# Lag rows of an S5 mixer fetched from on-chip copies in channel-first order, and the transforms of the last two units placed ahead of the late part

## Chip, core and metric

One NeuronCore of a Trainium2 chip runs the kernel; nothing is shared with another core. The metric is the device time of one execution in microseconds (us), the median over several runs. Engines: TensorE (PE; PEld is its weight load), VectorE (DVE), ScalarE (ACT), GpSimd (POOL), and SyncE (SP), which here only issues DMAs. ScalarE and GpSimd have DMA queues of their own.

## The reference, cut to what matters

One layer over 1024 latent tokens of width 1024 and 256 context tokens: a bidirectional S5 mixer with GELU and GLU, then a SwiGLU feed-forward net (FFN). Both have RMSNorm ahead and adaLN (shift, scale, gate, each a product of SiLU(c) with `ada_w`). The mixer has 64 groups of 16 channels, each with 64 complex states in each direction:

```python
def s5_direction(u_ctx, u_lat, lam_re, lam_im, log_step, b_re, b_im, c_re, c_im):
    lam_bar = jnp.exp(lam * jnp.exp(log_step)[:, None])
    b_bar = ((lam_bar - 1.0) / lam)[..., None] * lax.complex(b_re, b_im)
    c_mat = lax.complex(c_re, c_im)
    def run(u, h0):
        bu = jnp.einsum('lgh,gnh->lgn', u, b_bar)
        bu = bu.at[0].add(lam_bar * h0)
        _, h = lax.associative_scan(_linear_combine, (broadcast lam_bar, bu), axis=0)
        return jnp.einsum('lgn,ghn->lgh', h, c_mat).real, h[-1]
    y_c, h_c = run(u_ctx, 0)
    y_l, _ = run(u_lat, h_c)
    return y_c, y_l
# mixer: y = forward + backward + d_skip*h;  g = gelu(y);  g * sigmoid(g @ w_glu + b_glu)
# FFN:   (silu(h @ w1) * (h @ w3)) @ w2;     then the final RMSNorm
```

## The kernel before, in words

**Chunks of eight.** The sequence is cut into 128 chunks of T = 8 tokens. Within a chunk the output is a product of the chunk's inputs with a Toeplitz matrix of *lag kernels* (15 lags, -7 to 7, of 16 x 16 for each group); across chunks a recurrence runs over 128 chunk states. A chunk's input to one group is 8 x 16 = 128 numbers, and these stand on the 128 partitions: position s in the chunk times channel h, in the order s*16 + h. The 64 groups make eight *units* of eight groups, and two units a *quarter* q.

**Stages.** Up to about 123 us a preamble makes powers of lambda, the input matrices (`BL1`, `BL2`, made out of `LB` by `bl_make` and turned by `bl_tr`), the modulated input `U` and each chunk's contribution to the state. Then `scan` is the recurrence: VectorE steps from chunk to chunk, six operations a step, until 221 us. Beside it the other engines work through `PROG1`, a list written out by hand; from 222 us on all engines work through `PROG2`, then the GLU and the FFN. The order of the instructions on each engine is the order of the lists: an operation that waits holds up what stands behind it on its engine.

**Names in the lists** (the number is a unit 0-7, for T half a unit 0-15, for K half a quarter, for C a quarter and a part; `run` takes a list apart):
- `A`: products of adaLN with `ada_w`, whose tiles SP loads (L523). `M`, `m`: rows and columns made of them.
- `C`: readout factors of a quarter and direction on GpSimd (`cl_ops`): three products, L77, with two adds. `HOWS` says for each add how it is made: `P` on TensorE by two products with the identity and a copy (L693, L694), `Y` by an accumulating DMA issued on GpSimd (L696), `E` on GpSimd (L77). `q`, `G`, `L` prepare C; `q2` holds `pw_sums(1)` too.
- `K`: the lag kernels of half a quarter on TensorE (`k_mats`: L842, L846, L850), copied from PSUM to SBUF by ScalarE (L854) and from there written to the DRAM tensor `kd` (L855, 120 KB in 128 rows); `O` zeroes a PSUM tile first (L804).
- `T`: `toeplitz`, the fetch of the lag rows of four groups, half a unit, from `kd` to a tile of `KQ` (L863 on SP, 256 KB, 512 rows of 512 bytes). `KQ` has four tiles: a unit takes two of them, and the unit after the next takes the same two.
- `F`: GpSimd fills the odd chunk states of a quarter that the recurrence steps over.
- `R`, `Z`, `z`: copies of states in turned order for the backward direction (L955 on ScalarE, L957 on VectorE), of the first half of the chunks, the second half, and all.
- `P`: first half of a unit: `states_mm` (L975) for chunks that have both directions early, and `x_mm` (L999), the product of `U` with the lag rows, for all chunks; `Y`: its copy from PSUM (L1057, ScalarE). `N`: the second half's `states_mm`; `D`: its add on VectorE. Units 0 to 5 are done so.
- `Q`: units 6 and 7 instead have x_mm and `states_all` (L988), all chunks at once, in the late part, with no `D`.
- `H`: gelu on ScalarE (L1066, or L1069 in two halves straight from PSUM for 6 and 7); `I`, `J`: transposes for the GLU (L1123) with their copies (L1125) and low parts; `g`: the GLU's products (L1163); `w`, `l`, `W`, `V`: loads of `w_glu` (SP) and casts of it; `x`: gates.

All DMAs of SP's and ScalarE's queues share eight semaphores in turn, in the order of the program: each waits for the landing of the one eight before it. GpSimd's have eight of their own.

## Time and profile before

| what | us |
|---|---|
| runs, median (lowest to highest) | 1009.99 (1006.97 to 1013.54) |
| the profiled execution | 1006.91 |
| its span | 1005.1 |
| TensorE busy | 952.8 |
| GpSimd busy | 748.7 |
| end of the recurrence on VectorE | 221.1 |
| N0 to the first product of the GLU | 222.8 to 251.9 |

The span is what the profiler saw from the first to the last instruction; the execution's own time is 1.8 us longer, the median of the runs 3.1 us longer than that execution. A row of a grouped answer reads: line, engine, operation, out<-in by the program's names, shapes, count | busy us, mean ns of one | idle time of that engine just ahead of them and what ended it. A row of the timeline reads: start, duration, engine, line, operation, count, and in brackets the idle time ahead of it. A matmul in fp32 is recorded as two records. A row of a table of stretches gives, for each engine, busy us and records, then the granted TensorE clock (1.00 is full), the DMA engines' mean busy share, and GB/s.

### The profile page before, as it was taken

The numbers are of one execution on the slowest core, as the hardware profiler recorded it, in microseconds if no ns is written. First come the engines' busy times: TensorE is split into PE (matmuls) and PEld (weight loads), VectorE is DVE, ScalarE is ACT, GpSimd is POOL, SyncE is SP. The second block draws the span as 40 slices with busy tenths as digits, with TensorE's granted clock in tenths as the row PEclk, the third lists the DMA queues.
The fourth block names the chain that finished last, engine by engine and source line by source line (L and its number), as shares of the span: only waits on it lengthen the run. The fifth ranks groups of instructions, "written<-read, shape, count | busy, mean of one in ns | idle before, by whom it ended". The sixth has DMA issues, their size and how long they took to land. (4 is left out here: it accounts for less than half of the span.)

```text
span 1005.1 us, 17726 instructions
## 1 busy us (share of the span) xinstructions
PE 952.8 (95%) x6604; PEld 751.5 (75%) x6604; DVE 774.3 (77%) x1630; ACT 427.7 (43%) x808; POOL 748.7 (74%) x595
## 2 busy tenths in 40 slices
...
GB/s 335 285 133 108 287 316 273 125 85 171 210 64 22 1 105 84 11 43 42 74 53 74 42 79 34 47 61 45 74 42 84 43 64 32 61 55 53 74 22 167
DMA packets 49118, 99.95 MB, mean 99 GB/s; under 512 B 4348, under 2 KB 18940, under 8 KB 47752
## 3 DMA queue, kind: packets, MB, share of 16 engines
...
## 5 line engine op out<-in xcount | busy, mean ns | idle before, releaser
L77 POOL TENSOR_TENSOR c<-rxc,c 128x512 fp32r<-128x512 f32 x127 | 166.0, 1320 | 52.3 <-ACT c L1305 51.5
L1364 PE MATMUL ut<-ra,c 128*128 128x512 f32 x400 | 155.7, 389 | 1.2 <-DVE ra L77 1.2
L1363 PE MATMUL ut<-ra,c 128*128 128x512 f32 x400 | 155.7, 389 | 0.2 <-ACT ra L1305 0.2
L1365 PE MATMUL ut<-ra,c 128*128 128x512 f32 x400 | 155.6, 389 | 0.0
L1305 ACT CAST c<-rxc 128x512 fp32r<-128x512 f32 x128 | 79.0, 622 | 147.6 <-PE xt L1658 53.0
L1658 PE MATMUL xt<-c,c 128*128 128x512 f32 x540 | 129.7, 389 | 0.0
L77 DVE TENSOR_TENSOR ru<-ru,xt 128x1024 f32<-128x1024 f32 x90 | 107.9, 1216 | 13.4 <-PE xt L1658 9.4
L1658 PEld LDWEIGHTS xt<-c,c 128*128 128x128 f32 x540 | 101.4, 188 | 21.0
L77 DVE TENSOR_TENSOR ru<-ut,ru 128x512 f32<-128x512 f32 x98 | 67.2, 686 | 44.1 <-PE ut L1365 38.6
L1364 PEld LDWEIGHTS ut<-ra,c 128*128 128x128 f32 x400 | 75.1, 188 | 17.1 <-POOL rxc L77 1.5
L1363 PEld LDWEIGHTS ut<-ra,c 128*128 128x128 f32 x400 | 75.1, 188 | 16.1 <-ACT ra L1305 0.6
L1365 PEld LDWEIGHTS ut<-ra,c 128*128 128x128 f32 x400 | 75.1, 188 | 15.6
L77 POOL TENSOR_TENSOR c<-ru,c 128x512 fp32r<-128x512 f32 (+1 forms) x39 | 58.8, 1507 | 10.1 <-ACT c L1305 5.7
L77 POOL TENSOR_TENSOR rxc<-rxc 128x512 f32<-128x512 f32 (+1 forms) x44 | 63.8, 1450 | 2.2 <-ACT rxc L671 0.6
L77 POOL TENSOR_TENSOR c<-rw,c 128x512 fp32r<-128x512 f32 (+1 forms) x28 | 37.4, 1337 | 37.5 <-ACT c L1305 37.5
L1363 PE MATMUL ut<-c,c 128*128 128x512 f32 x160 | 62.3, 390 | 0.8 <-DVE rxa L77 0.8
L1364 PE MATMUL ut<-c,c 128*128 128x512 f32 x160 | 62.3, 389 | 0.0
L1365 PE MATMUL ut<-c,c 128*128 128x512 f32 x160 | 62.2, 389 | 0.0
L1658 PE MATMUL ut<-c,c 128*128 128x512 f32 x216 | 51.9, 389 | 0.0
L77 DVE TENSOR_TENSOR ru<-ru,ut 128x512 f32<-128x512 f32 x76 | 47.3, 680 | 0.7 <-ACT ru L1712 0.5
L1658 PEld LDWEIGHTS ut<-c,c 128*128 128x128 f32 x216 | 40.5, 188 | 8.4
L587 PE MATMUL pv<-ru,c 128*64 128x160 f32 x512 | 41.4, 312 | 5.2 <-ACT c L450 2.0
...
## 6 DMA issues: line engine op xcount, KB each, us to landing
c<-in_ada_w SPq DMA_DIRECT2D x46, 256.0 KB, 5.9
rxc<-in_w SPq DMA_DIRECT2D x38, 256.0 KB, 2.9
rxc<-in_w SPq DMA_DIRECT2D x19, 512.0 KB
c<-c POOLq DMA_DIRECT2D x11, 512.0 KB, 5.7
ru<-in_w SPq DMA_DIRECT2D x11, 512.0 KB
rw<-in_w SPq DMA_DIRECT2D x11, 512.0 KB, 3.6
ra<-in_ada_w SPq DMA_DIRECT2D x10, 512.0 KB, 10.8
ra<-in_ada_w SPq DMA_DIRECT2D x18, 256.0 KB, 8.8
```

The costliest lines, as they stand in the source:

```text
L77: eng.tensor_tensor(out=o, in0=x, in1=y, op=op)
L587: PE.matmul(pv[64 * (i % 2):64 * (i % 2) + 64, ri, c0:c0 + 160], w[:, i, 64 * ri:64 * ri + 64], U[:, 8 * b + 4 * j + i], start=True, stop= ...
L1305: S.copy(o[0], x)
L1363: PE.matmul(pu, wh, bh, start=start, stop=False)
L1364: PE.matmul(pu, wh, bl, start=False, stop=False)
L1365: PE.matmul(pu, wl, bh, start=False, stop=stop)
L1658: PE.matmul(pd, w[:, cs_], b, start=j in (1, 2, 4) and n == 0, stop=n == 2, skip_group_check=j not in (1, 2, 4))
```

## The change

1. **Channel-first order.** The 128 rows of a chunk's input stand as h*8 + s. The host arrays `xT`, `ctxT`, `blk` and `sel` are laid out so, `LB`, `BL1`, `BL2` have their last two dimensions exchanged, and the copies and transposes that read them take other strides. Counts and sizes of the instructions stay.
2. **Lag rows from SBUF.** The sixteen writes to `kd` are gone. `k_mats` copies the two halves' lag kernels into two SBUF tiles `KX`, and `toeplitz(u, hq, eng)` fetches from these: two DMAs a call, each for one group, 64 KB in 128 rows of 512 bytes; in channel-first order the destination's partitions follow from 16 source partitions and 8 lags. That makes 64 DMAs in place of 16 fetches and 16 writes. `T` and `t` (groups of the quarter's first and second K) issue on SP, `e0` to `e3` and `f0` to `f3` on ScalarE, right behind K0 and K1. Tiles of `KQ` are taken as before, so T12, T13, t12, t13 (unit 6) wait until P4 has read unit 4's, and T14, T15, t14, t15 (unit 7) until P5 has read unit 5's.
3. **Adds of the readout.** `HOWS` has two `E` in the third quarter and the `P` in the fourth replaced by `Y`. Signs are moved so that no `Y` add needs a sign after it. `pw_sums(1)` has two operations on GpSimd and one on ScalarE instead of four on GpSimd, as an entry of its own (`n1`) ahead of F10. C22 stands ahead of C21.
4. **Units 6 and 7.** `Q6`, `Q7` and the whole-length copies `z6`, `z7` go. `X6`, `X7` (their x_mm), the first halves `R6 S6 Y12 Y13`, `R7 S7 Y14 Y15` stand at the end of `PROG1`; `Z6 N6 D6`, `Z7 N7 D7` in `PROG2` make the second halves as for the other units, and one gelu of 128 x 1024 each replaces two.

The diff's core:

```diff
-HOWS = "YPYP EPEP YEYE YPYE"
+HOWS = "YPYP EPEP YYYY YYYE"
-PROG1 = ("A22 ... A34 K0 O1 A38 A42 C10 C11 K1 O2 L2 A46 A50 C12 C13 A54 K2 O3 A58 T0 T1 T2 T3 F10 F11 G2 R0 K3 L3 R1 P0 Y0 Y1 A64 M0 P1 T4 T5 R2 Y2 Y3 G3 q2 C20 T6 T7 C21 P2 R3 Y4 Y5 C22 M1 P3 Y6 Y7 C23 q3 C30 K4 K5 R4 T8 T9 T10 T11 C31 C32 C33 F30 F31 P4 R5 Y8 Y9 K6 P5 Y10 Y11 K7 T12 T13 T14 T15 w0 l1 M2 m0 w1")
+PROG1 = ("A22 ... A34 K0 e0 e1 e2 e3 O1 A38 A42 C10 C11 K1 O2 L2 f0 f1 f2 f3 A46 A50 C12 C13 n1 A54 K2 O3 A58 F10 F11 G2 R0 K3 L3 R1 P0 Y0 Y1 T4 T5 t4 t5 A64 M0 P1 R2 Y2 Y3 T6 T7 t6 t7 G3 q2 C20 C22 C21 P2 R3 Y4 Y5 M1 P3 Y6 Y7 C23 q3 C30 K4 T8 T9 T10 T11 K5 t8 t9 t10 t11 R4 C31 C32 C33 F30 F31 P4 R5 Y8 Y9 K6 T12 T13 K7 t12 t13 P5 Y10 Y11 T14 T15 t14 t15 w0 X6 X7 l1 M2 m0 w1 R6 S6 Y12 Y13 R7 S7 Y14 Y15")
-PROG2 = ("Z0 N0 Z1 Z2 D0 Z3 N1 D1 Z4 H0 H1 N2 D2 H2 N3 Z5 D3 H3 N4 D4 z6 z7 I0 J0 I1 J1 H4 N5 D5 I2 J2 H5 I3 J3 W0 W1 W2 W3 x0 x1 x2 x3 Q6 H6 I4 J4 Q7 I5 J5 V1 b0 w20 w21 l1 H7 g03 g13 ...")
+PROG2 = ("Z0 N0 Z1 Z2 D0 Z3 N1 D1 Z4 H0 H1 N2 D2 Z5 H2 N3 D3 Z6 H3 N4 Z7 D4 H4 I0 J0 N5 D5 I1 J1 H5 W0 W1 N6 D6 I2 J2 H6 I3 J3 W2 W3 x0 x1 x2 x3 N7 D7 I4 J4 H7 V1 b0 w20 w21 l1 I5 J5 g03 g13 ...")
...
-        LB = view(RC[2], 8, [2, T, P])
+        LB = view(RC[2], 8, [2, P, T])
...
-                    PE.transpose(pt[:, j, P * i:P * i + P], t1[:, 4 * j + i].rearrange("p s h -> p (s h)"), ident)
+                    PE.transpose(pt[:, j, P * i:P * i + P], t1[:, 4 * j + i].rearrange("p h s -> p (h s)"), ident)
...
-            tt(PS[i], PWF[:, :, 0, :, gs], PWF[:, :, 1, :, gs], ADD, E)
-            if i == 0:
-                tt(PWF[:, :, 1, :, gs], PWF[:, :, 1, :, gs], PWF[:, :, 0, :, gs], SUB, E)
-            else:
-                for d, gs, neg in ((slice(0, 2), slice(16, 24), True), (slice(0, 1), slice(24, 32), False), (slice(1, 2), slice(24, 32), True)):
-                    re, im = PWF[:, :, 0, d, gs], PWF[:, :, 1, d, gs]
-                    tt(im, re if neg else im, im if neg else re, SUB, E)
+            re, im = PWF[:, :, 0, :, gs], PWF[:, :, 1, :, gs]
+            tt(PS[i], im, re, SUB if i else ADD, E)
+            tt(im, im, re, ADD if i else SUB, E)
+            if i:
+                S.activation(im, im, AF.Copy, scale=-1.0)
...
-            tt(c2, c0, c1, SUB, E)
+            tt(c2, c0, c1, ADD if q > 1 else SUB, E)
...
-        KX = [cpk[:, HC + P:HC + P + 15 * HC], cols.rearrange("p a b g -> p (a b g)")[:, 0:15 * HC]]
-        KX += [view(RW, 4 + i, [15 * HC]) for i in range(2)]
+        KX = [R0[:, 32 + P:32 + P + 30 * HC], view(RW, 4, [30 * HC])]
+        KX = [t.rearrange("p (g x) -> p g x", g=2) for t in KX]
-        KD_ = [dr.tile([P, 4, 15 * HC], F32, tag=f"kd{q}", name=f"kd{q}") for q in range(4)]
...
-                gq, kx = 2 * hq + g_, KX[2 * hq + g_]
-                S.copy(kx, kts[g_])
-                S.dma_start(KD_[q][:, gq], kx)
-        def toeplitz(u):
-            q, gi = divmod(u, 4)
-            rows = KD_[q][32 * gi:32 * gi + HC]
-            n = 15 * HC
-            src = bass.AP(rows.tensor, rows.offset, [[HC, T], [n, 4 * HC], [1, P]])
-            SY.dma_start(KQ[u % 4], src)
+                S.copy(KX[hq][:, g_], kts[g_])
+        def toeplitz(u, hq, eng=SY):
+            for g_ in range(2):
+                rows = KX[hq][32 * (u % 4):32 * (u % 4) + HC, g_]
+                src = bass.AP(rows.tensor, rows.offset, [list(rows.ap[0]), [HC, T], [1, P]])
+                eng.dma_start(KQ[u % 4][:, 2 * hq + g_], src)
...
-        def states_all(k, pts, hs):
...
-        HSq = {6: view(RA, 0, [P, 2, 4]), 7: view(RA, STB, [P, 2, 4])}
...
-                    toeplitz(i)
+                elif op in "Ttef":
+                    toeplitz(i, int(op in "tf"), S if op in "ef" else SY)
...
-                    inner[i] = x_mm(i, pe8)
-                    states_all(i, inner[i], HSq[i])
+                elif op == "X":
+                    inner[i] = [pw([4, T, HC]), pw([4, T, HC]) if i == 6 else pm.rearrange("p (a t h) -> p a t h", a=4, t=T)]
+                    x_mm(i, inner[i], True)
+                elif op == "S":
+                    states_mm(i, inner[i], 0, HSe[i], False)
...
-                    if i in late:
-                        S.activation(Y[:, i], Y[:, i], AF.Gelu_apprx_tanh)
-                    else:
-                        for gp in range(2):
-                            S.activation(yview(i, gp), inner[i][gp], AF.Gelu_apprx_tanh)
+                    S.activation(Y[:, i], Y[:, i], AF.Gelu_apprx_tanh)
```

What this moves, at three places. In the changed kernel the same operations have other line numbers: L966 is the old L975 (states_mm), L975 the old L999 (x_mm), L1093 the old L1123 (transposes), L1133 the old L1163 (GLU), L850 the old L854, L1031 the old L1057, L946 the old L955, L857 the fetch.

First, TensorE from N0 to the GLU's first product. Before (a row of 64 L975 is two units):

```order
L975 MATMUL pe<-c_63,ra 64x128 x64
L975 MATMUL pe<-c_64,ra 64x128 x64
L975 MATMUL pe<-c_65,ra 64x128 x32
L1123 MATMUL pe<-r_60,ru 128x128 x8
L975 MATMUL pe<-c_65,ra 64x128 x32
L1123 MATMUL pe<-r_60,ru 128x128 x8
L999 MATMUL pe<-ra,ru 128x128 x8
L988 MATMUL pe<-c_66,ra 64x128 x64
L1123 MATMUL pe<-r_60,ru 128x128 x4
L999 MATMUL pe<-ra,ru 128x128 x8
L988 MATMUL pe<-c_66,ra 64x128 x64
L1123 MATMUL pe<-r_60,ru 128x128 x4
```

and in the changed kernel:

```order
L966 MATMUL pe<-c_63,ra 64x128 x64
L966 MATMUL pe<-c_64,ra 64x128 x64
L966 MATMUL pe<-c_65,ra 64x128 x32
L1093 MATMUL pe<-r_60,ru 128x128 x4
L966 MATMUL pe<-c_65,ra 64x128 x32
L1093 MATMUL pe<-r_60,ru 128x128 x4
L966 MATMUL pe<-c_66,ra 64x128 x32
L1093 MATMUL pe<-r_60,ru 128x128 x8
L966 MATMUL pe<-c_66,ra 64x128 x32
L1093 MATMUL pe<-r_60,ru 128x128 x8
L1133 MATMUL pe<-c_3321,c_3268 128x512
```

The two x_mm and the two whole state products are gone; two halves (c_66) stand in their place among the transposes.

Second, ScalarE behind K0 and K1. Before:

```order
L854 COPY r_60<-kt 128x240
L855 DMA kd_1250<-r_60 128x240
L854 COPY r_60<-pw 128x240
L855 DMA kd_1250<-r_60 128x240
L804 COPY pw<-r_60 128x240
L694 ACTIVATE c_64<-pw 128x512 x2
L854 COPY rw<-kt 128x240
```

and in the changed kernel:

```order
L850 COPY r_60<-kt 128x240
L850 COPY r_60<-pw 128x240
L857 DMA ra<-r_60 128x1x128 x8
L802 COPY pw<-r_60 128x240
L692 ACTIVATE c_64<-pw 128x512 x2
L850 COPY rw<-kt 128x240
L850 COPY rw<-pw 128x240
L802 COPY pw<-r_60 128x240
L665 DMA rxc<-in_cxy 128x512
L857 DMA ra<-rw 128x1x128 x8
L692 ACTIVATE c_64<-pw 128x512 x2
```

Eight issues of fetches stand ahead of the zeroing for K1 (L802), and eight more ahead of the second pair of copies of C's adds (L692).

Third, ScalarE at the end of `PROG1`, from K7's copies on, in the changed kernel:

```order
L850 COPY rw<-kt 128x240
L850 COPY rw<-pm 128x240
L1031 COPY ru<-pw 128x4x8x16 x2
L946 COPY ra<-ra 128x512
L1031 COPY ru<-pw 128x4x8x16 x2
L946 COPY ra<-ra 128x512
L1031 COPY ru<-pw 128x4x8x16
L1031 COPY ru<-pm 128x4x8x16
L946 COPY ra<-ra 128x512 x2
```

The copies of P5's result, R6, the copies of S6's result (Y12, Y13), R7, those of S7's (Y14, Y15), then the first copies of the late part on ScalarE (Z2, Z4). Before, K7's copies stood behind those of P5, and Z2 and Z4 right behind them.

70 lines of the change are left out of this document (26 added, 44 removed).

## The prediction

> **What bounds the kernel now.** I read the page first, then the table of stretches, then the stretch that the change shortens, group by group.
>
> ```profile
> span 1005.1 us, 17726 instructions
> PE 952.8 (95%) x6604; PEld 751.5 (75%) x6604; DVE 774.3 (77%) x1630; ACT 427.7 (43%) x808; POOL 748.7 (74%) x595
> ```
>
> 95% is an average over two regimes, which the stretches separate (each engine's busy us, then granted clock, DMA share, GB/s):
>
> ```profile
> 150.00:175.00 25.00, 21.97 (x563) 13.49 (x563) 25.00 (x144) 7.02 (x17) 22.12 (x26) 0.86 0.87 276
> 250.00:275.00 25.00, 25.00 (x166) 20.89 (x160) 11.70 (x12) 10.71 (x16) 19.21 (x10) 1.00 0.56 196
> ...
> 500.00:700.00 200.00, 200.00 (x884) 165.62 (x883) 141.71 (x169) 76.22 (x132) 156.47 (x118) 1.00 0.17 55
> ```
>
> Up to about 222 us VectorE is the bound: the recurrence, step after step, 25.00 busy of 25. From there on TensorE is: 200.00 of 200. The border is in the timeline of VectorE, followed there by the first copies of the late part (Z0, Z1):
>
> ```profile
> 220.82 0.29 DVE L77 TENSOR_TENSOR ra<-ltc,ra 128x128 f32<-128x128 f32 x1
> 221.25 0.76 DVE L957 COPY ra<-ra 128x512 f32<-128x512 f32 x2
> ```
>
> The late part begins with N0 (L975) and ends with the GLU's first product (L1163); by the answer on L975's line and by the timeline of TensorE:
>
> ```profile
> L975 PE MATMUL pe<-c,ra x384: 266/282/391, 222.8 to 237.2; 64*64 64x128 f32 x192
> ```
> ```profile
> 251.90 0.47 PE L1163 MATMUL pe<-c,c 128*128 128x512 f32 x1
> ```
>
> So a TensorE record taken out of 222.8–251.9 is worth its full time; one put in ahead of 222 costs nothing as long as TensorE is still through when the recurrence is. What that stretch holds, grouped by line (busy us, mean ns, idle before):
>
> ```profile
> L975 PE MATMUL pe<-c,ra 64*64 64x128 f32 x384 | 12.9, 285 | 1.3 <-issue 0.9 <-ACT rw L854 0.5
> L988 PE MATMUL pe<-c,ra 64*64 64x128 f32 x256 | 8.6, 288 | 0.4 <-issue 0.4
> L999 PE MATMUL pe<-ra,ru 128*128 128x128 f32 x32 | 3.9, 275 | 0.0
> L1123 PE MATMUL pe<-r,ru 128*128 128x128 f32 x24 | 3.5, 282 | 0.0
> ...
> ```
>
> 12.9 are N0 to N5, 8.6 and 3.9 are Q6 and Q7 whole, 3.5 the transposes; 29.1 us in all.
>
> **What the late part loses.** Q6 and Q7 go (8.6 + 3.9 = 12.5). N6 and N7 come: 128 records of the L975 kind, 12.9 × 128 / 384 = 4.3. Net **−8.2**, if TensorE stays fed: VectorE has two more pairs of adds (D6, D7; 4 × 0.69 = 2.8 us, against 6.6 of idle that it has before its adds), ScalarE one whole gelu (1.06) for each pair of half ones. From the same grouping:
>
> ```profile
> L77 DVE TENSOR_TENSOR ru<-pe,ru 128x512 f32<-128x512 f32 x12 | 7.7, 686 | 6.6 <-PE pe L975 6.5
> L1066 ACT ACTIVATE ru<-ru 128x1024 f32<-128x1024 f32 x6 | 6.4, 1061 | 4.1 <-DVE ru L77 3.9
> ```
>
> The turned copies of units 6 and 7 halve. I let the 1.7 us of idle stand. After 251.9 nothing is changed, and everything there waits for TensorE, so the end moves with the first GLU product. The w_glu loads are queued on SP behind the last lag fetch; SP is through with those fetches at 230 now (202.24 + 27.73 in its row below) and should be at 218 then, so they come earlier, too.
>
> **What the stretch ahead of it gains and loses.** X6, X7 and S6, S7 must now be done before N0. Their price: 3.9 (the L999 row) and 4.5 (128 records, first row below). What they replace and what room there is, TensorE in 190–222.8 by groups:
>
> ```profile
> L999 PE MATMUL pw<-ra,ru 128*128 128x128 f32 x45 | 7.8, 336 | 4.2 <-DMA ra<-kd 4.2
> L975 PE MATMUL pw<-c,ra 64*64 64x128 f32 x128 | 4.5, 287 | 0.0
> L693 PE MATMUL pw<-c,r 128*128 128x512 f32 x4 | 3.6, 1003 | 0.6 <-POOL c L77 0.6
> L693 PE MATMUL pw<-ra,r 128*128 128x512 f32 x4 | 2.9, 827 | 0.0
> ```
>
> The adds of the last readout product by TensorE (L693) go: about 6.0. That is 8.4 − 6.0 = 2.4 more work. The idle of that stretch is 6.7 (32.8 less 12.91, 6.84 and 6.33):
>
> ```profile
> 190.00:205.00 15.00, 12.91 (x353) 8.54 (x355) 15.00 (x86) 4.83 (x10) 14.25 (x10) 0.77 0.42 94
> 205.00:216.00 11.00, 6.84 (x147) 6.09 (x142) 10.79 (x59) 1.08 (x2) 10.77 (x14) 0.69 0.50 114
> 216.00:222.80 6.80, 6.33 (x287) 5.95 (x278) 5.85 (x30) 2.15 (x5) 3.12 (x7) 1.00 0.14 41
> ```
>
> So there is room, if the waits go. Why they are there: a lag kernel is written to DRAM, and the fetch of its rows waits for the landing.
>
> ```profile
> SPq L863 <- DMA kd<-r: 29.0, 2, 17.3
> L855 ACTq DMA_DIRECT2D kd<-r x8: 326/330/1498, 146.2 to 217.8; - x8
> DMA to landing us min/median/max: 2.7/3.3/5.0
> 202.24 27.73 SPq L863 DMA_DIRECT2D ra<-kd  x8
> PE pw L999 <- DMA ra<-kd: 4.2, 2, 3.6
> ```
>
> (SP's waits; the two kinds of kd; SP's timeline, eight fetches of 256 KB; TensorE's waits in 190–222.8.) The fetches for P4 and P5 go out from 202.24 on, and TensorE waits 3.6 for them at the longest. Now the fetch reads SBUF directly: no write, no landing in between. A new copy is 64 KB in 128 packets; nothing here has that form. Nearest is the write of 120 KB, also 128 packets: 0.33 us of issue and 2.7 to 5.0 to landing. I take 0.4 and 3; the lower bound is 2.7, the upper the old fetch. The rate while the last four of those run, in slices of 0.3 us from 225 on, is about 150 GB/s, 262 KB in 1.7 us, one after another:
>
> ```profile
> GB/s 6 27 0 0 0 55 17 9 0 137 174 174 176 140 132 119 147 114 193 137 116 150 126 164 164 225 176 241 251 207 224 203 215 241 253 239 246 205 423 410
> ```
>
> Step by step with these: the readout products on GpSimd come earlier. The third quarter loses two adds and gains two accumulating DMAs, the last one an add for a DMA:
>
> ```profile
> 175.54 2.02 POOL L77 TENSOR_TENSOR c<-rxc,rxa 128x1024 f32<-128x1024 f32 x1 [2.10 <-PE pm L534]
> 177.64 2.37 POOL L77 TENSOR_TENSOR c<-c,c 128x1024 f32<-128x1024 f32 x1
> ...
> 194.75 0.88 POOL L696 DMA_DIRECT2D c<-ra  x1 [0.30 <-POOL c L77]
> 204.94 2.35 POOL L77 TENSOR_TENSOR c<-c,rw 128x1024 f32<-128x1024 f32 x1
> ```
>
> Two adds of 2.37 less two issues of 0.88 + 0.30: 2.4 saved; one more DMA costs 1.2; and the 2.10 us of waiting ahead of 175.54 mostly go, since C22 is put ahead of C21. GpSimd ends the last product about 204 where it ended at 207.3. K4 stays near 191 and K5 near 195, since the landing of the last accumulation takes the place of the add:
>
> ```profile
> c<-c POOLq DMA_DIRECT2D x11, 512.0 KB, 5.7
> ```
>
> The fetches for P4 land about 201, eight us earlier. P4 and P5 are 2.2 of states and 2.0 of L999 each at full clock, a lag kernel about 2 (K7's copy starts at 222.39, P5's before it at 220.54; rows below). K6 needs the last accumulation, issued about 199.5, at 205 to 206. So P4 ends at 205 to 207, K6 at 207 to 208, K7 at 209 to 210.5, P5 at 213.5 to 215. **The last eight copies** (T14, T15, t14, t15) overwrite rows that P5 reads, so they go out only then: eight issues of 0.4 and 3 to landing, 219 to 221 for X7's end (X6 fits in between). S6: 2.2 (half of the 4.5). Then a wait that the order makes: R7, the turned copy that S7 reads, stands on ScalarE behind Y12 and Y13, and those wait for S6. From the timeline of ScalarE:
>
> ```profile
> 204.22 0.61 ACT L955 COPY ra<-ra 128x512 f32<-128x512 f32 x1
> ...
> 220.54 1.08 ACT L1057 COPY ru<-pw 128x512 f32<-128x512 f32 x2 [2.76 <-PE pw L999]
> 222.39 0.36 ACT L854 COPY rw<-kt 128x240 f32<-128x240 f32 x1 [0.78 <-PE pm L850]
> ```
>
> 1.08 + 0.61 and the signals: 1.9. S7: 2.2. So N0 starts at 220 + 2.2 + 1.9 + 2.2 = **226.3**, not 222.8: **+3.5**. Ends of it: 222.8 (recurrence and Z0 still last; a lower one isn't possible), and 238 if the copies cost what the old fetch did (the rival below).
>
> **The early copies** (e0–e3, f0–f3) are sixteen issues on ScalarE among the ada_w loads, where DMA share is 0.87. Each DMA waits for the one eight before it in program order, on whichever queue, and a load of 256 KB there takes 4.9 to land:
>
> ```profile
> c<-in_ada_w SPq DMA_DIRECT2D x13, 256.0 KB, 4.9
> ```
> ```profile
> 150.47 2.49 SPq L523 DMA_DIRECT2D c<-in_ada_w  x4
> ```
>
> The eighth e copy waits for a load issued about 150, which lands at 155. So ScalarE stands still behind e from 147 to 155 and, by the next loads, behind f from 158 to 164; with it the zeroing for K1, and K1 itself, some 4 us late. Cover: P0 needs no write's landing any more, and A64 comes at 176 as before. I cost it at nothing; without that cover it would be those 4 us on N0, and so on the end. The channel-first layout changes strides and no count or size in the preamble: nothing, ±1.
>
> **Sum.** The profiled execution took 1006.91: 1006.91 − 8.2 + 3.5 = 1002.2. The median of the runs is 1009.99, 3.1 above it, so the forecast as a median is **1005.3**. About 1% (10 us) is what a measurement of this kernel tells from no change.
>
> **A rule weighed.** TensorE's clock here is granted in stretches: 0.50 in this one, though busy 5.92 of 6.82, with the 3.6 us wait just ahead.
>
> ```profile
> 209.14:215.96 6.82, 5.92 (x111) 5.37 (x113) 6.82 (x41) 1.08 (x2) 6.58 (x11) 0.50 0.39 102
> L999 PE MATMUL pw<-ra,ru x32: 275/399/582, 209.4 to 220.4; 128*128 128x128 f32 x32
> ```
>
> The Trainium skill, page "TensorE: Matmul & The Clock Gate", Part 1, says that an idle window of about 3.4 us halves the clock and a busy one brings it back. That agrees with the 3.6 and the 0.50. It would speak against the change if the waits for the last copies and for R7 fell into one such window: N0 and N1 would run at half clock. The states' records hardly show it (287 ns in the mean with half-clock ones among them, 285 without), so by it the sum rises by under 1 us.
>
> **Rivals.**
>
> *All of it.* The copies land in 2.7, R7 gets through, N0 starts near 223 as before: 1009.99 − 8.2 = 1001.8. For it: 6.7 of idle against 2.4 of work. Against: X7 and S7 each have a wait of their own at the very end.
>
> *Eaten.* The 4 us of ScalarE's standstill aren't covered, and N0 starts at 229 to 231: 1008 to 1010, no difference. For it: TensorE's order is fixed, and K1 to K3 already stand close before P0.
>
> *The other side: a small copy costs what a large one did.* If a copy's time is per transfer and not per byte, eight take 8 × 1.7 = 14 us after 215 and 3 more to the last landing, X7 ends at 232, N0 starts at 238: 1009.99 − 8.2 + 15 = 1017. It decides from N0 at 231 on. Against: the sixteen writes of 128 packets, at 2.7 to 5.0, don't show such piling up. The Trainium skill, page "DMA: Bandwidth & Descriptors", Rules for kernel authors, asks to coalesce small transfers, since under 64 KB one pays mostly overhead; no run here shows it, and the copies stand just at that size.
>
> **How the numbers follow.** Forecast (N0 at 224 to 228) 0.45, all of it 0.22, eaten 0.18, the other side 0.10, and 0.05 that something here gives more, such as clock regained in 195–216. Range: 997 (all of it, less the spread of the runs) to 1013 (eaten, and the near part of the other side). Faster by over 1% takes 10.1 us, more than "all of it" gives: a quarter of that case by spread, the 0.05, a little of the forecast: 0.14. Slower by over 1%: most of the other side: 0.08. Within: 0.78.
>
> **What would show it.** In the new profile: no kd rows; the stretch from N0 to the first GLU product 20 to 21.5 us instead of 29.1 (term one); N0 at 225–227 with a wait of S7 on ScalarE's copy just ahead and one of X7 on the copies (term two); ScalarE idle behind its DMA issues at 147–155. I am wrong if N0 starts at 223 or after 229, if the late stretch isn't shortened by 8, or if the gain is given back after the GLU.

## The result, and the profile after

The changed kernel takes 1023.62 us (median of 4 runs, 1022.32 to 1027.86), the kernel before, on the same chip, 1008.48 (1005.27 to 1013.54): ratio 1.0164, 95% interval [1.0136, 1.0193] (the quotient of the two medians alone is 1.0150). It is slower by some 15 us by the medians and 16 by the ratio; forecast were 1005.3 and no difference. The profiled execution took 1024.70.

First the page of the changed kernel and its table of stretches (busy us of PE, PEld, DVE, ACT, POOL; then granted clock, DMA share, GB/s):

```profile
span 1022.9 us, 17792 instructions
PE 954.3 (93%) x6596; PEld 752.2 (74%) x6596; DVE 779.1 (76%) x1634; ACT 432.2 (42%) x811; POOL 746.5 (73%) x594
```
```profile
200.00:225.00 25.00, 16.23 (x522) 13.86 (x522) 21.70 (x111) 4.62 (x10) 18.50 (x19) 0.66 0.57 97
225.00:250.00 25.00, 18.00 (x394) 15.84 (x398) 0.00 (x0) 5.35 (x12) 2.38 (x6) 0.86 0.61 161
250.00:275.00 25.00, 25.00 (x560) 23.10 (x557) 18.43 (x26) 15.21 (x20) 12.21 (x9) 1.00 0.04 13
```

TensorE's total is the same to 1.5 us (952.8 before), so the time came in as waiting. Its place is the row 225–250: VectorE does nothing at all there (0.00), since the recurrence is over, and TensorE is busy 18.00 of 25 at a clock of 0.86. Before, VectorE had its first late copies at 221.25. From 250 on TensorE is full again. So the time was lost ahead of the late part, in the stretch in which the prediction saw room.

Where the late part lies now, by the answers on two lines' records and the timeline of TensorE:

```profile
L966 PE MATMUL pe<-c,ra x512: 271/282/390, 248.9 to 268.4; 64*64 64x128 f32 x171
L966 PE MATMUL pw<-c,c x128: 270/284/493, 174.9 to 197.6; 64*64 64x128 f32 x128
```
```profile
269.50 0.47 PE L1133 MATMUL pe<-c,c 128*128 128x512 f32 x1
```

The `pe` records of L966 are N0 to N7, the `pw` ones with `c,c` are half of the records of P0 to P3. N0 starts at 248.9, the first GLU product at 269.50: 20.6 us, against 29.1. The grouping of that stretch by line has no row of Q6 and Q7 (the old L988 and L999) any more; its largest is this one:

```profile
L966 PE MATMUL pe<-c,ra 64*64 64x128 f32 x510 | 17.0, 285 | 0.5 <-ACT ru L1031 0.5
```

Now the way to N0. The records on tile `kt` are K4's and K5's (min, median, max ns, first and last start), before and then after:

```profile
L842 PE MATMUL kt<-c,rxa x64: 256/256/391, 191.3 to 195.8; 64*16 64x112 f32 x64
```
```profile
L839 PE MATMUL kt<-c,rxa x64: 363/391/391, 206.9 to 213.1; 64*16 64x112 f32 x64
```

and the states of P4 and P5, by the answers on their line, before and after:

```profile
L975 PE MATMUL pw<-c,ra x128: 270/282/389, 203.6 to 218.5; 64*64 64x128 f32 x128
```
```profile
L966 PE MATMUL pw<-c,ra x128: 397/414/492, 215.1 to 234.3; 64*64 64x128 f32 x128
```

| us | before | after | the piece's growth |
|---|---|---|---|
| P0 starts | 168.0 | 174.9 | +6.9 |
| K4 starts | 191.3 | 206.9 | +8.7 (P0 to K4: 23.3, now 32.0) |
| N0 starts | 222.8 | 248.9 | +10.5 (K4 to N0: 31.5, now 42.0) |
| first GLU product | 251.9 | 269.5 | −8.5 |

26.1 lost, 8.5 won: 17.6 of the span's 17.8. Each of the three lost pieces has its own waits.

**Up to P0.** ScalarE's timeline at the early copies (issuing instructions, with their whole stay), and the waits in 140–176:

```profile
147.97 7.91 ACTq L857 DMA_DIRECT2D ra<-r  x8
155.92 0.36 ACT L802 COPY pw<-r 128x240 f32<-128x240 f32 x1 [7.72 <-DMA ra<-r]
159.38 8.39 ACTq L857 DMA_DIRECT2D ra<-rw  x8
167.86 1.08 ACT L692 ACTIVATE c<-pw 128x512 f32<-128x512 f32 x2 [8.18 <-DMA ra<-rw]
```
```profile
POOL rxc L77 <- ACT rxc L669: 6.0, 1, 6.0
PE pw L839 <- ACT pw L802: 3.1, 1, 3.1
PE kt L839 <- ACT c L692: 2.6, 1, 2.6
```

Eight copies hold ScalarE for 7.91 and 8.39 us; behind them stand the zeroing for K1 (TensorE waits 3.1), ScalarE's part of a readout product (2.6) and its sign operation for the third one (L669; GpSimd waits 6.0 for it).

**P0 to K4.** DMA in 177–207, before and after: queues with packets, MB and share of the 16 engines' time; then issues with the KB of each and the median us from issue to landing. q0 holds the accumulations (L694 on GpSimd), q1 the copies (L857):

```profile
q0 software_dynamic: 490, 1.77, 32.4%
```
```profile
q0 software_dynamic: 947, 3.49, 62.6%
q1 hardware_dynamic: 2312, 1.06, 24.8%
...
c<-c POOLq DMA_DIRECT2D x4, 512.0 KB, 7.1
ra<-r SPq DMA_DIRECT2D x8, 64.0 KB, 4.3
ra<-rw SPq DMA_DIRECT2D x8, 64.0 KB, 6.6
```

3.49 MB of accumulations are some 6.7 of 512 KB; 62.6% of 30 us is 18.8 us of all sixteen engines, so 2.8 us each. (Before, by the first row, it is 32.4% for 1.77 MB, or 3.4 of them: 2.9 each.) Beside them a copy lands in 4.3 to 6.6 us. With nothing beside them (211–226, same kernel) the same copies land in 2.4 to 2.6:

```profile
ra<-r SPq DMA_DIRECT2D x9, 64.0 KB, 2.6
ra<-rw SPq DMA_DIRECT2D x8, 64.0 KB, 2.4
```

SP's timeline shows the queue, four issues to a row: 3.86 and 5.17 us for four beside the accumulations, 2.5 at the end.

```profile
177.68 3.86 SPq L857 DMA_DIRECT2D ra<-r  x4
190.11 5.17 SPq L857 DMA_DIRECT2D ra<-r  x4
...
235.21 2.48 SPq L857 DMA_DIRECT2D ra<-r  x4
237.74 2.52 SPq L857 DMA_DIRECT2D ra<-rw  x4
```

TensorE's waits in 176–250 (sum, number, longest):

```profile
PE pw L975 <- DMA ra<-rw: 10.5, 7, 2.8
PE pm L847 <- issue: 4.3, 3, 2.0
PE pw L966 <- ACT ra L946: 2.2, 2, 1.5
```

The first row is mostly P2 and P3 waiting for copies ahead of K4 (9.4 us in 189–207); the rest is P4's (0.2) and, behind P5, that for the last copies (0.9). Before, the same 176–250 had 5.0 of such waits:

```profile
PE pw L999 <- DMA ra<-kd: 5.0, 3, 3.6
```

**K4 to N0.** The clock in the rows of these waits and behind them is low, and K4 to P5 run through it (stretches, columns as above):

```profile
195.00:207.00 12.00, 6.01 (x88) 5.04 (x92) 11.79 (x63) 0.71 (x3) 11.03 (x9) 0.78 0.87 152
207.00:216.00 9.00, 5.99 (x293) 5.03 (x292) 9.00 (x53) 1.93 (x6) 3.11 (x3) 0.50 0.33 56
...
226.00:237.00 11.00, 7.91 (x220) 7.14 (x215) 0.00 (x0) 1.16 (x4) 1.39 (x5) 0.69 0.35 55
```

The median record of the states takes 414 ns instead of 282, K4's 391 instead of 256. From K4's start to P5's end it is 30.0 us (206.9 to 236.9), where the prediction had 22 to 24; from P5's end to N0 it is 12.0, where the prediction had 12 (its middle, 214.3, to 226.3).

### The profile page after: what moved, and what is told of

Same layout as the page of the kernel before. It is cut to its first block, busy times and chain, and to the rows that moved or that the text cites. A ratio compares the mean times of both kernels' runs of the same rounds, so it can differ in the third digit from the quotient of the medians.

```text
span 1022.9 us, 17792 instructions
## 1 busy us (share of the span) xinstructions
PE 954.3 (93%) x6596; PEld 752.2 (74%) x6596; DVE 779.1 (76%) x1634; ACT 432.2 (42%) x811; POOL 746.5 (73%) x594
## 3 DMA queue, kind: packets, MB, share of 16 engines
q1 hardware_dynamic: 42008, 85.60, 26.1%
q10 hardware_dynamic: 3024, 1.82, 0.7%
## 5 line engine op out<-in xcount | busy, mean ns | idle before, releaser
L77 POOL TENSOR_TENSOR c<-rxc,c 128x512 fp32r<-128x512 f32 x127 | 165.8, 1318 | 52.4 <-ACT c L1275 51.5
L77 DVE TENSOR_TENSOR ru<-ru,xt 128x1024 f32<-128x1024 f32 x90 | 107.5, 1215 | 11.8 <-PE xt L1628 8.4
L77 DVE TENSOR_TENSOR ru<-ut,ru 128x512 f32<-128x512 f32 x98 | 67.2, 686 | 44.1 <-PE ut L1335 38.7
L77 POOL TENSOR_TENSOR rxc<-rxc 128x512 f32<-128x512 f32 (+1 forms) x44 | 64.1, 1456 | 7.6 <-ACT rxc L669 6.0
L77 POOL TENSOR_TENSOR c<-rw,c 128x512 fp32r<-128x512 f32 (+1 forms) x28 | 38.3, 1368 | 37.7 <-ACT c L1275 37.7
L77 POOL TENSOR_TENSOR c<-ru,c 128x512 fp32r<-128x512 f32 (+1 forms) x39 | 57.7, 1480 | 10.1 <-ACT c L1275 5.7
L77 DVE TENSOR_TENSOR ru<-ru,ut 128x512 f32<-128x512 f32 x76 | 47.2, 680 | 0.3
## 6 DMA issues: line engine op xcount, KB each, us to landing
rxc<-in_w SPq DMA_DIRECT2D x19, 512.0 KB, 3.7
c<-c POOLq DMA_DIRECT2D x13, 512.0 KB, 6.4
ru<-in_w SPq DMA_DIRECT2D x11, 512.0 KB, 7.5
rw<-in_w SPq DMA_DIRECT2D x11, 512.0 KB, 3.6
ra<-in_ada_w SPq DMA_DIRECT2D x10, 512.0 KB, 10.8
```

Source lines behind the costliest of these rows:

```text
L77: eng.tensor_tensor(out=o, in0=x, in1=y, op=op)
```

## The experiments

Three theories, each with its place. **A**: the early copies hold ScalarE, and P0 comes late. **B**: the accumulating DMAs fill the DMA engines, the copies land late behind them, and TensorE waits and loses its clock. **C**: X6, X7, S6 and S7, with the last copies and R7 ahead of them, cost more before N0 than Q6 and Q7 cost after it. In the table all runs, as a ratio (with its 95% interval) to the kernel before on the same chip, with the three starts from each one's profiled execution. A start is one execution's: e2, e8, e10, e11 and e14 have the same lists up to P0, and theirs lie between 171.4 and 175.4, so differences of P0 of up to 4 us prove nothing by themselves.

| kernel | median us | ratio, interval | P0 | N0 | GLU |
|---|---|---|---|---|---|
| before | 1008.48 | | 168.0 | 222.8 | 251.9 |
| after | 1023.62 | 1.0164 [1.0136, 1.0193] | 174.9 | 248.9 | 269.5 |
| e1, early copies on SP | 1024.53 | 1.0164 [1.0122, 1.0207] | 178.5 | 252.2 | 272.9 |
| e2, old adds | 1012.24 | 1.0055 [1.0039, 1.0071] | 171.7 | 236.2 | 256.2 |
| e3, both of these | 1017.59 | 1.0092 [1.0068, 1.0117] | 179.6 | 242.9 | 263.2 |
| e4, old late part | 1017.84 | 1.0110 [1.0079, 1.0141] | 172.1 | 232.0 | 262.2 |
| e5, new late part alone | 1020.37 | 1.0139 [1.0105, 1.0174] | 170.0 | 244.7 | 264.5 |
| e6, e2 with early copies later | 1015.60 | 1.0083 [1.0058, 1.0109] | 175.2 | 240.0 | 261.4 |
| e7, new adds alone | 1011.52 | 1.0054 [1.0035, 1.0073] | 170.3 | 231.6 | 261.5 |
| e8, e2 with another end | 1014.69 | 1.0059 [1.0039, 1.0078] | 175.4 | 238.6 | 260.4 |
| e9, copies alone | 1007.51 | 1.0011 [0.9995, 1.0027] | 173.3 | 227.2 | 254.6 |
| e10, e2 with R7 first | 1012.40 | 1.0051 [1.0031, 1.0070] | 171.4 | 234.1 | 255.7 |
| e11, e8 with SP's issues | 1009.35 | 1.0003 [0.9985, 1.0020] | 174.5 | 234.1 | 254.7 |
| e12, e9 with K7 later | 1006.67 | 0.9979 [0.9954, 1.0004] | 175.2 | 224.9 | 253.4 |
| e13, e12 with K4 ahead of P3 | 1005.30 | 0.9978 [0.9963, 0.9994] | 173.8 | 221.9 | 251.1 |
| e14, e11 with K4 ahead of P3 | 1007.04 | 0.9990 [0.9971, 1.0009] | 172.1 | 230.6 | 251.8 |

### The early copies moved to SP (e1, e3)

```diff
-K0 e0 e1 e2 e3 O1
+K0 T0 T1 T2 T3 O1
...
-L2 f0 f1 f2 f3 A46
+L2 t0 t1 t2 t3 A46
```

> The changed kernel with its sixteen early copies (e0 to e3, f0 to f3) issued on SP at the same places of the list, so ScalarE no longer stands behind them. Theory A (ScalarE's standstill of 8 us behind e and 8 us behind f is what makes everything late): K2 starts at about 160 instead of 168.5, P0 at 168 to 170 instead of 174.9, GpSimd's third quarter at 168 instead of 172.6, and the whole is 5 to 7 us faster than the changed kernel's 1023.6: about 1017. Theory B (copies and accumulating DMAs get in each other's way in 177 to 207): P0 is earlier, but the same copies meet the same accumulations, P2 and P3 wait the longer, and under 2 us is gained: about 1022.

No gain: 1.0164 as before the edit. ScalarE is free now, but SP stands behind the same copies, and SP issues the ada_w loads. TensorE's waits in 150–185:

```profile
PE pm L534 <- DMA ra<-in_ada_w: 2.6, 1, 2.6
```

P0 starts at 178.5. A's remedy in this form only changes whose queue stands still. With the old adds it was the same:

```diff
-HOWS = "YPYP EPEP YYYY YYYE"
+HOWS = "YPYP EPEP YEYE YPYE"
...
-K0 e0 e1 e2 e3 O1
+K0 T0 T1 T2 T3 O1
...
-L2 f0 f1 f2 f3 A46
+L2 t0 t1 t2 t3 A46
```

> Both edits: early copies on SP and the adds as before. If A and B each hold for their part, the gains add up: 1013 to 1016. If A alone holds it is no better than the early copies on SP alone (1017 or more); if B alone, no better than the old adds alone (1020 to 1022).

1.0092 against e2's 1.0055: SP is the worse place, P0 at 179.6 against 171.7.

### The old adds (e2), and the adds alone (e7)

```diff
-HOWS = "YPYP EPEP YYYY YYYE"
+HOWS = "YPYP EPEP YEYE YPYE"
```

> The changed kernel with the adds of the readout as before (the third quarter's two adds on GpSimd again, the fourth quarter's on TensorE again): two accumulating DMAs fewer in the third quarter, one fewer in the fourth. Theory B: of the 9.4 us for which P2 and P3 wait for copies in 189 to 207 at most half is left, K4 starts at about 202 instead of 206.9, and after the 6 us of TensorE adds (some of it in idle time) the whole is 1 to 4 us faster: 1020 to 1022. Theory A: the standstill is as before, the waits hardly change, the TensorE adds come on top: 1024 to 1029.

One line, 11.4 us: the median falls from 1023.62 to 1012.24, more than the 1 to 4 that B had expected. This is more than half of the loss, and the DMA view of e2 in 177–207 shows how:

```profile
q1 hardware_dynamic: 3362, 1.54, 36.2%
q0 software_dynamic: 510, 1.83, 32.9%
...
ra<-r SPq DMA_DIRECT2D x14, 64.0 KB, 2.4
ra<-rw SPq DMA_DIRECT2D x10, 64.0 KB, 4.8
```
```profile
PE pw L975 <- DMA ra<-rw: 2.6, 3, 1.0
```

Accumulations take 32.9% of the engines instead of 62.6; the copies of the first half land in 2.4 instead of 4.3 and those of the second in 4.8 instead of 6.6 (in e2 eight copies more lie in that stretch); TensorE's waits for copies (second fence, 176–250) fall from 10.5 to 2.6. The same sixteen copies compared, T4 to T7 and t4 to t7, show it best. In e2 the first eight still meet two accumulations: SP needs 4.73 and 5.24 us for four, and they land after 5.5. The other eight meet none:

```profile
186.08 2.53 SPq L857 DMA_DIRECT2D ra<-r  x4
188.66 2.54 SPq L857 DMA_DIRECT2D ra<-rw  x4
```

These land after 2.4 and 2.5; in the changed kernel the same eight, beside accumulations, take SP 5.17 and 4.43 and land after 4.3 and 5.5. K4 starts at 193.7 instead of 206.9; P0 to K4 takes 22.0 instead of 32.0. GpSimd isn't the cause: its last readout add starts at 206.92 in the changed kernel, at 204.44 in e2, only 2.5 apart, where K4 is 13 apart.

What e2 does not shorten is K4 to N0: 42.5, against 42.0 in the changed kernel and 31.5 before. Its clock there is 0.88 instead of 0.75, but TensorE has its adds back (3.1 + 2.9 us), and it is idle as long (10.4 of 42.5, 10.3 of 42.0). The accumulations show in the way up to K4; the growth behind it comes with the new late part, for without that K4 to N0 takes 31.4 (e9) and 29.6 (e4, both below).

The opposite way, the kernel before with part 3 alone:

```diff
-HOWS = "YPYP EPEP YEYE YPYE"
+HOWS = "YPYP EPEP YYYY YYYE"
...
-... C12 C13 A54 ... C20 T6 T7 C21 P2 R3 Y4 Y5 C22 M1 ...
+... C12 C13 n1 A54 ... C20 T6 T7 C22 C21 P2 R3 Y4 Y5 M1 ...
...
+            re, im = PWF[:, :, 0, :, gs], PWF[:, :, 1, :, gs]
+            tt(PS[i], im, re, SUB if i else ADD, E)
+            tt(im, im, re, ADD if i else SUB, E)
+            if i:
+                S.activation(im, im, AF.Copy, scale=-1.0)
```

> The kernel before with part three alone: three more accumulating DMAs, the signs moved, the sums ahead of F10, C22 ahead of C21; lag rows by way of DRAM, units 6 and 7 as before. If accumulations hurt only together with the 64 small copies: within 3 us of before. If they hurt any transfer that runs beside them, the old fetches and the landing that K4 waits for too: 5 to 11 us slower.

1.0054, so the adds cost without any copies, too. DMA in 178–200, and TensorE's and GpSimd's rows beside it:

```profile
q0 software_dynamic: 670, 2.43, 59.5%
c<-c POOLq DMA_DIRECT2D x3, 512.0 KB, 10.2
```
```profile
PE pw L997 <- DMA ra<-kd: 8.8, 2, 6.0
```
```profile
192.54 2.01 POOL L77 TENSOR_TENSOR c<-rxc 128x1024 f32<-128x1024 f32 x1 [3.73 <-DMA c<-c]
```

59.5% of 22 us for 2.43 MB (4.6 of 512 KB) is 13.1 us, again 2.8 each. The accumulations land 10.2 after their issue, the old fetches hold TensorE 6.0 at the longest, and GpSimd waits 3.73 for its own accumulation. (This profiled execution, 1016.06, was the slowest of its ten; the sizes are upper ones, the median is the time to go by.) B holds, with the old fetch and with the new.

### The old late part (e4), the new one alone (e5), the copies alone (e9)

e4 is the changed kernel with Q6 and Q7 back and X6 to S7 out:

```diff
-... t14 t15 w0 X6 X7 l1 M2 m0 w1 R6 S6 Y12 Y13 R7 S7 Y14 Y15
+... t14 t15 w0 l1 M2 m0 w1
...
-PROG2 = ("Z0 N0 ... Z6 H3 N4 Z7 D4 ... N6 D6 ... N7 D7 ...")
+PROG2 = ("Z0 N0 ... N4 D4 z6 z7 ... Q6 H6 I4 J4 Q7 ...")
```

> The changed kernel with units 6 and 7 in the late part as before (Q6, Q7, z6, z7 back; X, S and Y12 to Y15 gone). Theory C (the work moved ahead of N0 lies on the path there, since TensorE reaches the end of its early list only at 237): N0 starts at about 237 instead of 249.7, the late part takes 29 instead of 19.8, the whole is about 3.5 us faster: 1020. The opposite view, by which the moved work is free ahead of N0 and only the late part counts: 8 to 9 us slower, 1032.

1017.84, 5.8 less than with the new late part. N0 comes 16.9 earlier than in the changed kernel (232.0) and the late part is 9.6 longer (30.2 for 20.6): C is right in sign, though N0 comes 5 us earlier than it said.

e5 has the reverse, the kernel before with part 4 alone:

```diff
-... T14 T15 w0 l1 M2 m0 w1
+... T14 T15 w0 X6 X7 l1 M2 m0 w1 R6 S6 Y12 Y13 R7 S7 Y14 Y15
...
-PROG2 = ("Z0 N0 ... N4 D4 z6 z7 ... Q6 H6 I4 J4 Q7 ...")
+PROG2 = ("Z0 N0 ... Z6 H3 N4 Z7 D4 ... N6 D6 ... N7 D7 ...")
```

> The kernel before with part four alone: X6, X7 and the first halves of units 6 and 7 ahead of the late part, lag rows still by way of DRAM, adds as before. Theory C (what is moved ahead lies on the path, since the last lag rows come late): the last fetches land at 236.7 as before, X7 ends at about 239, N0 starts at about 244 instead of 222.8, the late part takes 20 instead of 29: 12 us slower than before, about 1019. If the moved work were free: 8 us faster, 999.

1.0139. The late part is 19.8, but with the old way of fetching, which writes to DRAM and reads back, X6 and X7 wait as the other x_mm do (7.9 of these 12.9 us, in 222–245, are theirs):

```profile
PE pw L983 <- DMA ra<-kd: 12.9, 4, 7.7
```

e9 is e4 with the old adds. That is the kernel before with parts 1 and 2 and, of part 3, what is not `HOWS`: the sums at `n1`, C22 ahead of C21, the signs:

```diff
-HOWS = "YPYP EPEP YYYY YYYE"
+HOWS = "YPYP EPEP YEYE YPYE"
```

> The kernel before with parts one and two alone: lag rows copied on chip, channel-first order; adds and units 6 and 7 as before. Theory B (it is copies and accumulations together that cost): 9 to 11 us faster than fetch only with the new adds (1017.8), so about 1008, no different from before. If the 64 copies cost by themselves, 1012 to 1016.

1.0011 [0.9995, 1.0027]: the copies by themselves, with these small moves, change nothing that can be measured. Differences of the ratios give each part's price (in % of the time before; for the adds, e7 has all of part 3, the differences `HOWS` alone):

| part | without the others | beside the copies | beside copies and the other |
|---|---|---|---|
| copies (parts 1, 2) | +0.1 (e9) | | |
| adds (part 3) | +0.5 (e7) | +1.0 (e4 − e9) | +1.1 (after − e2) |
| late part (part 4) | +1.4 (e5) | +0.4 (e2 − e9) | +0.5 (after − e4) |

From before over e9 and e4 to after that is 0.1 + 1.0 + 0.5 = 1.6%; a chain of differences adds up to the whole by itself. The intervals are some 0.2 to 0.4 wide to either side, so that the adds cost about double beside the copies is likely and not certain; both use the DMA engines in the same 30 us. The copies cut the late part's price to about a third; TensorE's waits for lag rows are 12.9 in e5 and 2.6 in e2.

### The early copies later (e6)

e2 with the copies placed behind C11 and C13, so that the zeroing for K1 no longer stands behind them:

```diff
-K0 e0 e1 e2 e3 O1 A38 A42 C10 C11 K1 O2 L2 f0 f1 f2 f3 A46 A50 C12 C13 n1
+K0 O1 A38 A42 C10 C11 e0 e1 e2 e3 K1 O2 L2 A46 A50 C12 C13 f0 f1 f2 f3 n1
```

> The changed kernel with the adds as before (1012.2) and the early copies still on ScalarE, but e0 to e3 behind C11's copies and f0 to f3 behind C13's, so that the zeroing for K1 and the copies that K2 needs no longer stand behind them. If ScalarE's standstill costs what shows on TensorE there (3.0 ahead of K1 and 2.6 ahead of K2), P0 starts 2 to 3.5 us earlier and the whole is 2 to 3.5 us faster: about 1009. If the next copies on ScalarE are merely held up instead, no difference: 1012.

A miss: 1015.60, and by the ratio 0.3% more than e2 with overlapping intervals, so no gain. The standstill has only moved: it now holds up the lag kernels' copies (L850) on ScalarE, for which TensorE waits 3.2 and 2.2 us in 140–180. With e1 and e3 this is the third form of A's remedy that gains nothing. Copies issued on GpSimd, whose eight semaphores are its own, were not tried. In the kernels without early copies P0 starts at 168.0 to 170.3, in those with them on ScalarE at 171.4 to 175.4; that they delay P0 by some us is seen, but none of the runs takes the delay away, and what it is worth at the end stays open.

### The end of the list (e10, e8, e11)

e10 is e2 with both turned copies ahead of both state products, which takes S7's wait for R7 away:

```diff
-R6 S6 Y12 Y13 R7 S7 Y14 Y15
+R6 R7 S6 S7 Y12 Y13 Y14 Y15
```

> The changed kernel with the adds as before (1012.2) and one edit: R7 ahead of Y12 and Y13 (and S7 ahead of them). The wait of 1.5 us for ScalarE's turned copy ahead of S7 goes: N0 1.5 us earlier, 1010.7. If the copies of S6 and S7 then hold up N0's banks instead, no difference.

N0 starts at 234.1 instead of 236.2, and the median is the same (1012.40, 1012.24): the 2 us are there in N0 and come back out before the GLU (21.6 for 20.0), 1.6 of them as one wait without a releaser.

e8 is e2 with P5 ahead of K7, so that the last copies go out earlier, half of them on ScalarE, and with the states ahead of x_mm (P6, P7 in place of X and S):

```diff
-K6 T12 T13 K7 t12 t13 P5 Y10 Y11 T14 T15 t14 t15 w0 X6 X7 l1 M2 m0 w1 R6 S6 Y12 Y13 R7 S7 Y14 Y15
+K6 T12 T13 P5 Y10 Y11 T14 T15 K7 t12 t13 R6 R7 f14 f15 w0 l1 M2 m0 w1 P6 P7 Y12 Y13 Y14 Y15
...
-                    inner[i] = [pw([4, T, HC]) for _ in range(2)]
+                    inner[i] = [pw([4, T, HC]), pw([4, T, HC]) if i < 7 else pm.rearrange("p (a t h) -> p a t h", a=4, t=T)]
```

> The changed kernel with the adds as before (1012.2), its early copies where they were, and a new order of what ends the early list: P5 ahead of K7, T14 and T15 behind P5, R6 and R7 ahead, the copies t14 and t15 on ScalarE beside SP's, units 6 and 7 with their states first and the x_mm behind (so that the states cover the landing of the last copies), their four copies from PSUM last. Theory C (the end of that list is a chain of waits that its order makes): N0 starts 5 to 9 us earlier than in the old-adds run (234.8+1.8), at 228 to 231, the whole takes 1004 to 1007, no slower than before. If it is TensorE's work that fills the stretch, not its waits: at most 2 us, 1010 to 1012.

A miss, 1.0059. The copies issued by ScalarE meet the w_glu loads that SP has just issued, and land 8.2 us after their issue, SP's copies in the same stretch (205–240) after 2.5:

```profile
ra<-rw SPq DMA_DIRECT2D x12, 64.0 KB, 2.5
...
ra<-rw ACTq DMA_DIRECT2D x4, 64.0 KB, 8.2
```

The Trainium skill, page "DMA: Bandwidth & Descriptors", section "Issuing engines are not separate DMA queues", says that transfers from all issuing engines run on the same 16 DMA engines and interleave; these rows agree, with 8.2 us on ScalarE's queue beside SP's loads. So e11 puts them on SP ahead of the loads:

```diff
-K7 t12 t13 R6 R7 f14 f15 w0 l1 M2 m0 w1 P6 P7
+K7 t12 t13 t14 t15 w0 l1 M2 m0 w1 R6 R7 P6 P7
```

> The new end of the list again, but with t14 and t15 on SP ahead of the w_glu loads instead of on ScalarE (where they went out beside those loads and landed up to 8 us after issue). All else as there: adds as before, P5 ahead of K7, states of units 6 and 7 ahead of their x_mm. If the last copies' waits were all that was left: X7 ends at 229 to 231, N0 starts there, the first GLU product comes at about 250, the whole takes 1005 to 1008, the same as before. If the early list is late for other reasons (P0 at 175 as in that run): 1010 to 1012.

1.0003 [0.9985, 1.0020], N0 at 234.1, GLU at 254.7: with the old adds and this end, the whole new late part costs nothing that can be measured, and wins nothing.

### The lag kernels apart (e12, e13), and all of it (e14)

One row of the changed kernel is without a releaser: 4.3 us of "issue" inside the lag kernels (L847), where the kernel before has 0.6. In e9 it is 2.7 in 212–226, in K7, which stands right behind K6 there. e12 is e9 with P5 between them:

```diff
-K6 T12 T13 K7 t12 t13 P5 Y10 Y11 T14 T15 t14 t15
+K6 T12 T13 P5 Y10 Y11 T14 T15 K7 t12 t13 t14 t15
```

> On-chip copies with the adds as before and units 6 and 7 in the late part (1007.5), and K7 behind P5 as in the kernel before, instead of straight behind K6. TensorE waited 3.4 us inside K7 there for nothing that the profile shows; if two lag kernels in a row outrun TensorE's instruction supply, the waits inside K7 fall under 1 us, N0 starts at 223 to 224.5 instead of 227.2, and the whole takes 1004 to 1005, faster than before by 2 to 3. If the waits come from something else (copies in flight), they stay: 1007.

e13 is e12 with P3 between K4 and K5 as well:

```diff
-M1 P3 Y6 Y7 C23 q3 C30 K4 T8 T9 T10 T11 K5
+M1 C23 q3 C30 K4 P3 Y6 Y7 T8 T9 T10 T11 K5
```

> The last version (on-chip copies, adds as before, K7 behind P5) with K4 ahead of P3, so that no two lag kernels stand straight behind one another any more. If two in a row outrun TensorE's instruction supply, the 3.3 us of waits inside K4 and K5 that the profile gives no releaser for fall under 1.5, the adds of the last readout start about 2 us earlier, N0 starts at 222.5 to 224 and the whole takes 1004 to 1006. If those waits come from the copies in flight, they stay where they are, 1006.7. If K4 now waits for GpSimd's third quarter ahead of P3, P3 is later by that wait and nothing is gained: 1007 to 1008.

The waits of e9 (212–226), of e12 (170–226, where what is left is K4's and K5's) and of e13 (176–226):

```profile
PE pm L847 <- issue: 2.7, 1, 2.7
```
```profile
PE pm L847 <- issue: 3.3, 2, 1.8
```
```profile
...
PE pe L967 <- DVE ra L77: 2.0, 1, 2.0
PE pm L847 <- issue: 1.7, 1, 1.7
```

K7's wait goes when P5 stands between (2.7 to none), and K4's and K5's fall from 3.3 to 1.7 when P3 does. But that a lag kernel follows another isn't the condition: what went in e13 is the wait inside K4 (1.82, ahead of 200.70 in e12), which had P3 in front; K5, now parted from K4, keeps its own (1.46 in e12, 1.67 in e13); and in the kernel before, where K5 follows K4 directly, the longest such wait of the two is 0.4. e13 is at 0.9978 [0.9963, 0.9994], the only version whose interval lies below one, and only just; its ratio is that of e12 (0.9979), so K4's move gains nothing that can be measured. It also shows the floor: TensorE waits 2.0 us for the recurrence ("DVE ra L77") just before N0 at 221.9. So for the copies without the new late part there is little more to win here: VectorE is the bound again.

e14 puts the same order under the whole change except for the adds (e11 with K4 ahead of P3):

```diff
-M1 P3 Y6 Y7 C23 q3 C30 K4 T8 T9 T10 T11 K5
+M1 C23 q3 C30 K4 P3 Y6 Y7 T8 T9 T10 T11 K5
```

> K4 ahead of P3 and K7 behind P5 as in the last run, and units 6 and 7 ahead of the late part as in the new end of the list on SP; adds as before. TensorE reached N0 at 219.9 in the last run and waited 2.0 us for the recurrence. If the moved work pays as soon as the waits ahead of it are gone: 8.4 us of it less the 2.0, and 1 to 2 of waits for the last copies, N0 at 228 to 230; the late part 20 to 21 instead of 29; GLU at 248 to 251, 1002 to 1005, 0 to 3 faster than the last run's 1005.3. If the last copies' waits grow by what the rest became faster (they go out only behind P5 and K7): N0 at 231 to 233, 1006 to 1008, and the move does not pay even then.

0.9990 [0.9971, 1.0009], no difference. N0 starts at 230.6 and the GLU at 251.8: 8.7 us later and 8.0 us shorter than e13's 221.9 and 29.2. The two cancel.

## Why the prediction was wrong

**The late part loses 8.2: right.** Measured 8.5 (29.1 to 20.6), in e5 9.3 (29.1 to 19.8), and nothing was given back after the GLU: span and first GLU product moved by 17.8 and 17.6.

**"2.4 saved" on GpSimd, K4 near 191, fetches for P4 landed about 201: this step failed.** It priced an accumulating DMA as GpSimd's time, 0.88 + 0.30 of issue. What it costs is 2.8 us of all sixteen DMA engines, and the fetches of the lag rows have to pass through the same engines in the same stretch. They landed after 4.3 to 6.6 instead of 3, K4 started at 206.9, and GpSimd, whose time was saved on paper, ended its last product at 209.3 (206.92 + 2.36) where 204 was forecast and 207.3 measured before. e2 shows it by the removal of these adds alone: 11.4 of 15.1 us, by the medians. The row on which the step stood, "x11, 512.0 KB, 5.7", gave a latency; the share of the engines in that stretch (0.87 DMA share at 150–175) was quoted for the early copies only.

**Early copies cost "nothing" under the cover of A64 at 176: wrong in size.** The standstill came as foreseen (147.97 to 155.9; 159.38 to 167.8 where 158 to 164 was said), but P0 moved by 6.9 (by 4.1 in e4, with the same lists up to there), and the stretch behind it has no slack once accumulations fill it. That GpSimd, too, would wait behind the standstill (6.0, for the sign operation of the third product) wasn't in the working. How much of the 6.9 reaches the end isn't settled.

**Half clock "under 1 us": wrong.** The prediction said that the states' records hardly show it, going by the kernel before. But there the states of P4 and P5 (203.6 to 205.9, 216.5 to 218.8) had a clock of 1.00: they lie on either side of the stretch at 0.50, and their mean of 287 ns says nothing of half clock. P4's x_mm was in that stretch; its row has a median of 399 ns and a least of 275. With one wait after another ahead of K4 the clock was 0.50 in 207–216 and 0.69 in 226–237. TensorE's timeline has the longest of these waits ahead of this row, and one of 2.16 behind it:

```profile
202.83 1.22 PE L975 MATMUL pw<-ra,ru 128*128 128x128 f32 x8 [2.83 <-DMA ra<-rw]
```

The Trainium skill, page "TensorE: Matmul & The Clock Gate", Part 1, puts the idle window that halves the clock at about 3.4 us; here no single wait was that long, but in 195–207 half of the time was idle (6.01 busy of 12), and the clock went all the same. P5's 64 records took 3.7 us (231.0 to 234.3 for the starts, and one record) instead of 2.3; two units, with the lag kernels at 391 ns for 256, and the 3.7 more of "issue" waits make up the most of the 6 to 8 us by which K4 to P5's end missed.

**N0 at 226.3 (+3.5): its own working was right, its start was not.** From P5's end to N0 the copies, X7, S6, the wait for R7 and S7 took 12.0 us, as worked out; S7's wait for R7 was 1.55 where 1.9 was said. But it started at 236.9 instead of 214. And since the recurrence was over by 225, this chain lay wholly on the path, where the prediction had set most of it against TensorE's 6.7 us of idle under VectorE. (The adds that it took off, 6.0, are 6.5 by its own rows; this weighs little.) That is theory C, and the reason why even e14 gains nothing: Q6 and Q7 were 12.5 us of TensorE after N0; X6, X7, S6, S7, N6, N7 are 3.9 + 4.5 + 4.3 = 12.7, of which 8.4 is now ahead of N0, in a stretch that has room for it only while VectorE is still busy.

**The rivals.** "The other side" named the right sign and nearly the right size (N0 at 238, 1017), by a mechanism that is not there: a small copy alone lands in 2.4 to 2.6 and four are issued in 2.5, so eight need some 5 us and not 14. "Eaten" named the right place, ScalarE, for 6.9 us. No rival spoke of the DMA engines' time that the accumulations take.
